# The norm sums of the input read from a second, token-major load, and the start of attention put in another order

## The chip, the cores and the metric

The kernel runs on one core of one Trainium2 chip. The metric is the device time of one execution in microseconds (us); the profile is one execution taken by the hardware profiler. The engines are TensorE (PE for its matmuls, PEld for its weight loads), VectorE (DVE), ScalarE (ACT), GpSimd (POOL) and SyncE (SP), which here only issues transfers. Each engine works through its instructions strictly in order; an instruction that waits holds back all behind it on that engine. A smaller time is better.

## The reference

One decoder block on a 1024 x 1024 input (1024 tokens, 1024 features), in float32:

```python
h = rmsnorm(x, g_mix_pre)                        # x * rsqrt(mean(x*x, -1) + 1e-6) * g
proj = h @ w_in + b_in                           # 512 pool | 512 q | 128 k | 128 v | 2048 gates
y_pool = multiscale_pool(u_pool, w_pool) * pool_scale      # windows 2, 4, 8, 16
q, k = partial_rotary(q), partial_rotary(k)      # first 16 of 64 dimensions of each head
y_attn = sliding_window_sink_attention(q, k, v)  # 8 query heads, 2 kv heads, window 128
merged = sigmoid(g0) * (y_pool @ w_branch_pool) + sigmoid(g1) * (y_attn @ w_branch_attn)
x = x + rmsnorm(merged @ w_out, g_mix_post)
x = x + rmsnorm(square(relu(rmsnorm(x, g_mlp_pre) @ w_up)) @ w_down, g_mlp_post)
```

Only the first two lines and the start of the attention matter for the change: `rmsnorm` needs, for each token, the sum of the squares of its 1024 features.

## The kernel before

**Precision.** A float32 operand is split into a high part (a cast to fp32r, on ACT) and a low part (the difference, on DVE); a product is then three matmul passes, high x high, high x low, low x high (`PASSES`, L32). `split` (L99) does both halves: its ACT cast is recorded as L101, its DVE subtraction as L104.

**The projection loop (L205 to L242).** x is loaded feature-major (`xt`, features on the partitions), 128 features per step k of 8. Step k loads `xs` (512 KB, four buffers of the tag `s4`) and 768 columns of weights `ws` (384 KB, three staging buffers `st`), multiplies `xs` by the gain and splits it (L227 on ACT, L228 on DVE, once for each half of the tokens), splits the query and the key/value weights, and multiplies: tokens 0 to 511, that is the token tiles n = 0 to 3 of 128 tokens, for the queries (`mm_q`, L183) and the keys and values (`mm_kv`, L192). That is 24 matmuls per step. The norm is not applied to x: the rows of the result are multiplied by the inverse root `r1` later. For it, each step also squares its `xs` in place on ACT (L235; step 0 writes the running sum `sq` directly, L233), and POOL adds the square to `sq` (L236; the last of the seven additions is on DVE). `xs` is free for the next load after that addition.

**After the loop (L722 on).** `sq` holds sums over 8 features for each partition; 16 small matmuls against a column of ones (L725, eight in the program, each recorded twice) finish the sum per token into `bss`, laced with the query matmuls of token tile 4. `rsqrt` (L106) makes `r1` from it. `pre_qkv(n)` (L255) then takes tile n out of PSUM with `r1` and the bias (L260, L261, DVE) and does the rotary part (L268 to L271: on DVE for n = 0, on POOL else). `post_qkv(n)` (L280) transposes it on PE (L289, L290) and splits it into query and key tiles for `score` (L312, matmuls L328). 

**What sets the order.** Up to L721 a scheduler with estimated times orders every engine. From L722 PE, DVE and ACT keep the written order, while the SP and POOL queues are still ordered by the scheduler. Between the pieces of the attention `fill(t)` (L643) takes t microseconds' worth, by estimate, of independent PE work from the generator `others` (L606): the query and key/value projections of the token tiles 4 to 7, then the pool branch's `u` projections (L574) and the product of `w_pool` with the branch weights (L594). `between` and `late` hold ACT and DVE work that belongs to that stream and is emitted at certain points of it. The stream takes its PSUM banks from three of the tag `mm`; token tile 5 gets the bank in which token tile 2's queries stood, so its first matmul needs `pre_qkv(2)`.

After the attention (about 178 us on) come the gate projections, the output projection, and the two MLP products, which the change does not touch.

Of the kernel before, what the change touches and what calls it, by code (L numbers as in the profile page):

```python
# [8 lines left out]
F32 = mybir.dt.float32  # L9
# [5 lines left out]
P = 128  # L15
S = 1024
# [26 lines left out]
V_BU = V_G + 8  # L43
V_BG = V_BU + 4
V_PS = V_BG + 16
V_ONE = V_PS + 4
V_N = V_ONE + 1


@with_exitstack  # L50
def block_kernel(ctx: ExitStack, tc, xt, x, consts, vecs, sinks, b_qkv, g_post, g_mlp, g_mlp_post,
# [94 lines left out]

    cst = cp.tile([P, C_N], F32, name="cst")
    vec = cp.tile([P, V_N], F32, name="vec")
    snk = cp.tile([P, NH], F32, name="snk")
    nsnk = cp.tile([P, NH], F32, name="nsnk")  # L150
    r1 = cp.tile([P, NT], F32, name="r1")
# [44 lines left out]
    bq01 = bank("sc", [2, 512])  # L196
    bq = {0: bq01[:, 0, :], 1: bq01[:, 1, :], 2: bank("mm"), 3: bank("mm")}
    bkv = {0: bank("at", [2, 256]), 2: bank("at", [2, 256])}
    bss = bank("at", [NT])
    bz = bank("mm")  # L200
    for j in range(11):
        pe.matmul(bz, zeros[:, 0, :P], zeros[:, 0, :], start=j == 0, stop=j == 10)
    sq = at("qkv", 3, [S])
    ones = vec[:, V_ONE:V_ONE + 1]
    for k in range(NK):  # L205
        xs = at("s4", 4, [S])
        ws = stage([768]) if k else ws_first
        if k < 2:
            nc.sync.dma_start(xs[:, :512], xt[k][:, :512])
            if k:  # L210
                nc.sync.dma_start(ws, w_qkv[k])
            else:
                nc.sync.dma_start(vec, vecs)
                nc.sync.dma_start(ws[:, 512:], w_qkv[k][:, 512:])
            nc.sync.dma_start(xs[:, 512:], xt[k][:, 512:])
        else:
            nc.sync.dma_start(xs, xt[k])
            nc.sync.dma_start(ws, w_qkv[k])
        halves_ = [xp.tile([P, 2, 512], F32R, tag="x", name=nm("x")) for _ in range(2)]
        gk = vec[:, V_G + k:V_G + k + 1]  # L220
        q = wslot([2, 512]) if k < 6 else ga_.tile([P, 2, 512], F32R, tag="ga", name=nm("wq"))
        if k % 2 == 0:
            wkv.append(ga_.tile([P, 2, 2, 256], F32R, tag="ga", name=nm("wkv")))
        kv = wkv[-1]
        for th, t in enumerate(halves_):
            c = slice(th * 512, (th + 1) * 512)
            act.activation(t[:, 0, :], xs[:, c], AF.Identity, scale=gk)  # L227
            dve.scalar_tensor_tensor(t[:, 1, :], xs[:, c], gk, f32(t[:, 0, :]), ALU.mult, ALU.subtract)  # L228
            if th == 0:
                split(q[:, 0, :], q[:, 1, :], ws[:, :512])  # L230
                split(kv[:, 0, k % 2, :], kv[:, 1, k % 2, :], ws[:, 512:])
        if k == 0:
            act.activation(sq, xs, AF.Square)  # L233
        else:
            act.activation(xs, xs, AF.Square)  # L235
            (pool if k < NK - 1 else dve).tensor_tensor(sq, sq, xs, ALU.add)  # L236
        xs_.append(halves_)
        wq.append(q)
        for n in range(4):
            mm_q(n, k, bq[n])  # L240
        for n in range(4):
            mm_kv(n, k, joint=True)  # L242
    nc.sync.dma_start(cst, consts)
    nc.sync.dma_start(snk, sinks.unsqueeze(0).broadcast_to([P, NH]))
    bq_b = bcast(b_qkv, 768)
# [290 lines left out]
    def flush(todo):  # L536
        while todo:
            todo.pop(0)()
# [67 lines left out]
    def others():  # L606
        for n in range(4, NT):
            flush(late)
            bq[n] = bank("mm")
            for k in range(NK):  # L610
                mm_q(n, k, bq[n])
                yield 3 * 0.227
            if n == NT - 1:
                load_u(3)
                flush(between[1])
            bkv[n] = bank("at" if n == 4 else "mm", [1, 256])
            for k in range(NK):
                mm_kv(n, k)
                yield 3 * 0.12
            if n == 4:  # L620
                late.append(lambda: pre_qkv(4))
            else:
                pre_qkv(n)
        wps = stage([4, P])
        nc.sync.dma_start(wps, w_pool)
        between[0].append(lambda: split(wpt[:, 0], wpt[:, 1], wps))
        wpt = bcp.tile([P, 2, 4, P], F32R, tag="bc", name="wpt")
        wpts.append(wpt)
        for gi in (3, 2, 1, 0):
            load_wb(gi)  # L630
            if gi:
                load_u(gi - 1)
            yield from u_half(gi, 0)
            if gi < 3:
                yield from wb_half(gi + 1, 1)
            yield from u_half(gi, 1)
            yield from wb_half(gi, 0)
        yield from wb_half(0, 1)
# [81 lines left out]

    LOW, HIGH = range(4), range(4, 8)  # L721
    with tc.manual_schedule(engines={mybir.EngineType.PE, mybir.EngineType.DVE, mybir.EngineType.Activation}):  # L722
        for n in range(NT):
            fill(0.34)
            pe.matmul(bss[:, n:n + 1], sq[:, n * P:(n + 1) * P], ones, start=n == 0, stop=n == NT - 1)  # L725
        rsqrt(r1, bss[:, :NT], NT)
        act.activation(warm, r1[:, :1], AF.Exp)
        pre_qkv(0)
        pre_qkv(1)
        fill(5.4)  # L730
        post_qkv(0)
        pre_qkv(2)
        fill(2.8)
        score(0, 0)
        score_prev(0, 0)
# [627 lines left out]
def _layout(inputs):  # L1363
# [18 lines left out]
    for col, t in ((C_COS, np.cos(ang)), (C_SIN, np.sin(ang))):  # L1382
# [4 lines left out]
        b_in[:512].reshape(4, P).T,  # L1387
        b_in[1280:].reshape(16, P).T,
        a["pool_scale"][0].reshape(4, P).T,
        np.ones((P, 1), f),  # L1390
    ], axis=1)
    return [
        ("xt", c(x.T).reshape(NK, P, S)),
# [39 lines left out]
```

## Time and profile before

| | us |
|---|---|
| median of 3 runs | 1133.97 (1133.69 to 1134.46) |
| the profiled execution, its own time | 1134.51 |
| its span from first to last instruction | 1132.7 |
| PE busy | 1114.8 |
| DVE busy | 820.6 |
| ACT busy | 526.7 |
| POOL busy | 77.8 |
| mean granted TensorE clock | 0.996 |

The span is 1.8 us shorter than the execution's time; what is saved inside the span is taken off the time. In a row of the timeline the first number is the start in us, the second the duration; `x12` means that twelve equal instructions were merged, and a bracket gives the idle time just before and what ended it. In a row of groups the numbers behind the bar are the total busy time in us, the mean in ns, and the idle time of the engine just before its members. Windows give, for a stretch, the busy time of each engine, the granted clock, the share of the transfer engines and GB/s. PE's busy time contains slow stretches and modelled ends, so starts of instructions are compared rather than busy shares.

### The profile page before, as it was taken

To read this page: it belongs to the slowest core of one execution; us is meant where nothing else is said; L and a number is where in the kernel's file an instruction comes from. 1 tells how busy PE (TensorE), PEld (TensorE's weight loads), DVE (VectorE), ACT (ScalarE), POOL (GpSimd) and SP (SyncE) were. 2 spreads that over 40 slices of the span, in tenths; PEclk is the share of its full clock that TensorE was granted. 3 is DMA by queue.
4 is the path that set the end of the run, shared out by engine and by line. 5 is a ranking of instruction groups with operands and counts; after the bars stand their busy time and mean duration, and the time that the engine had idled before them with its cause. 6 is when DMAs were issued, how large, how long until landed. Compare 5 with 4: busy or idle time off the path is not lost.

```text
span 1132.7 us, 14023 instructions
## 1 busy us (share of the span) xinstructions
PE 1114.8 (98%) x5183; PEld 920.9 (81%) x5183; DVE 820.6 (72%) x1210; ACT 526.7 (47%) x912; POOL 77.8 (7%) x111
## 2 busy tenths in 40 slices
PE   8999999999999999999999999999999999999997
PEld 7888778888888888888788888888888888888885
DVE  7668857899858885678998666666457955446787
ACT  6445655544432333446555444444444345344342
POOL 2443211000000330000000000000000000000000
PEclk9999999999999999999999999999999999999999
DMA  7205669366664444243365343434597765332652
GB/s 248 84 1 110 151 138 285 117 224 220 211 236 141 143 158 154 94 149 112 121 230 202 145 160 141 164 139 167 214 337 266 242 203 189 110 93 75 215 192 94
DMA packets 80179, 189.02 MB, mean 167 GB/s; under 512 B 6896, under 2 KB 19312, under 8 KB 80112
## 3 DMA queue, kind: packets, MB, share of 16 engines
q1 hardware_dynamic: 70144, 166.38, 43.8%
q10 hardware_dynamic: 5616, 19.66, 4.5%
q0 software_dynamic: 4352, 2.10, 1.8%
q8 instruction: 40, 0.66, 0.2%
q14 instruction: 27, 0.22, 0.1%
HBM read 132.54 MB, written 55.57 MB: 166 GB/s over the span
## 4 chain that ended last, share of the span: by engine, by line
PE 87%; DVE 7%; ACT 3%; DMA 2%; issue 1%; SPq 0%; DVEq 0%; ACTq 0%
PE mm L484 22%; PE at L484 16%; PE at L1270 14%; PE mm L1270 12%; PE mm L987 6%; PE mm L421 5%; PE mm L183 3%; PE mm L423 3%; PE mm L574 2%; PE at L987 1%; PE at L192 1%; DVE wh L104 1%; PE at L392 1%; PE sc L328 1%; DMA st<-in_w_up_dram 1%
## 5 line engine op out<-in xcount | busy, mean ns | idle before, releaser
L1270 PE MATMUL at<-ar,wh 128*128 128x512 f32 x744 | 169.6, 389 | 0.0
L1270 PEld LDWEIGHTS at<-ar,wh 128*128 128x128 f32 x744 | 139.6, 188 | 29.3 <-DVE ar L104 0.4
L1270 PE MATMUL mm<-ar,wh 128*128 128x512 f32 x576 | 131.0, 389 | 0.0
L1270 PEld LDWEIGHTS mm<-ar,wh 128*128 128x128 f32 x576 | 108.1, 188 | 22.5
L104 DVE TENSOR_TENSOR wh<-raw,wh 128x1024 fp32r<-128x1024 f32 x53 | 64.8, 1223 | 83.4 <-ACT wh L101 83.4
L101 ACT CAST wh<-raw 128x1024 fp32r<-128x1024 f32 x53 | 55.8, 1053 | 133.9 <-PE at L1270 60.3
L101 ACT CAST wh<-st 128x512 fp32r<-128x512 f32 (+1 forms) x105 | 66.3, 642 | 84.6 <-PE at L484 29.9
L104 DVE TENSOR_TENSOR wh<-st,wh 128x512 fp32r<-128x512 f32 (+1 forms) x105 | 81.8, 789 | 29.6 <-ACT wh L101 27.1
L484 PE MATMUL mm<-gr,wh 128*128 128x512 f32 x309 | 74.2, 390 | 0.0
L484 PE MATMUL mm<-T,wx 128*128 128x512 f32 x288 | 67.6, 389 | 0.0
L484 PEld LDWEIGHTS mm<-gr,wh 128*128 128x128 f32 x309 | 57.8, 188 | 11.8
L484 PEld LDWEIGHTS mm<-T,wx 128*128 128x128 f32 x288 | 54.1, 188 | 11.2
L484 PE MATMUL at<-T,wx 128*128 128x512 f32 x252 | 59.1, 389 | 0.0
L484 PEld LDWEIGHTS at<-T,wx 128*128 128x128 f32 x252 | 47.3, 188 | 9.8
L484 PE MATMUL mm<-x,wh 128*128 128x512 f32 x240 | 55.2, 389 | 0.0
L484 PEld LDWEIGHTS mm<-x,wh 128*128 128x128 f32 x240 | 45.1, 188 | 9.3
L104 DVE TENSOR_TENSOR ar<-B,ar 128x1024 fp32r<-128x1024 f32 x37 | 45.1, 1219 | 6.6 <-ACT ar L101 6.4
L574 PE MATMUL mm<-x,wh 128*128 128x512 f32 x192 | 47.6, 396 | 0.0
L101 ACT CAST ar<-B 128x1024 fp32r<-128x1024 f32 x37 | 38.9, 1050 | 8.8 <-DMA B<-in_w_dn_dram 6.0
L484 PE MATMUL at<-gr,wh 128*128 128x512 f32 x174 | 42.3, 390 | 0.0
L574 PEld LDWEIGHTS mm<-x,wh 128*128 128x128 f32 x192 | 35.2, 188 | 7.8
L484 PEld LDWEIGHTS at<-gr,wh 128*128 128x128 f32 x174 | 32.6, 188 | 7.2 <-DVE gr L104 0.5
(362 smaller groups left out, 2188.3 us busy)
## 6 DMA issues: line engine op xcount, KB each, us to landing
raw<-f_dram SPq DMA_DIRECT2D x53, 512.0 KB, 3.8
f_dram<-g SPq DMA_DIRECT2D x30, 512.0 KB, 3.3
B<-in_w_dn_dram SPq DMA_DIRECT2D x24, 512.0 KB, 6.6
st<-in_w_up_dram SPq DMA_DIRECT2D x22, 512.0 KB, 3.7
st<-in_w_g_dram SPq DMA_DIRECT2D x18, 512.0 KB, 4.2
f_dram<-g ACTq DMA_DIRECT2D x17, 512.0 KB, 2.6
g<-spill_dram SPq DMA_DIRECT2D x16, 512.0 KB, 4.4
raw<-in_w_dn_dram SPq DMA_DIRECT2D x16, 512.0 KB, 4.6
```

The source lines that it names most:

```text
L101: act.copy(hi, src)
L104: eng.tensor_tensor(lo, src, f32(hi), ALU.subtract)
L183: pe.matmul(bq, xs_[k][n // 4][:, xh, n % 4 * P:(n % 4 + 1) * P], wq[k][:, h, :], start=k == 0 and j == 0, stop=k == NK - 1 and j == 2)
L192: pe.matmul(bkv_of(n), xs_[k][n // 4][:, xh, n % 4 * P:(n % 4 + 1) * P], wkv[k // 2][:, h, k % 2, :], start=k == 0 and j == 0 and not (joi ...
L328: pe.matmul(sb[:, kv, i, :nk], qt[r, qx, m * P:(m + 1) * P], kx[r, k0:k0 + nk], start=j == 0, stop=j == 2)
L392: pe.matmul(flat(yb), v[:, kv, :], flat(p[:, 4 * kv:4 * kv + 4]), start=j == 0, stop=j == len(mms) - 1)
L421: pe.matmul(bs[th], whi[:, k, :], rhs(k, hl, th), start=k == 0 and hl == 0, stop=False)
L423: pe.matmul(bs[th], wlo[:, k, :], rhs(k, 0, th), start=False, stop=k == nk - 1)
L484: pe.matmul(b, w[:, wh, kt, :], xo[kt][:, xh, :], start=not after and kt == 0 and j == 0, stop=kt == 3 and j == 2, skip_group_check=after)
L574: pe.matmul(b, (whi, wlo)[h][:, k, :], xr(k, xh, th), start=j == 0, stop=j == len(mms) - 1)
L987: pe.matmul(obs[n][dj], l, wos[k][whl][:, dj * 512:(dj + 1) * 512], start=k == 0 and hl == 0 and whl == 0, stop=k == NK - 1 and hl == 1)
L1270: pe.matmul(bs[t], fo[fh][:, k2, t * P:(t + 1) * P], wo_[wh][:, k2, :], start=not after and s2 == 0 and k2 == 0 and j == 0, stop=s2 == NS ...
```

## The change

- The squares no longer come from `xs`. A new helper `token_square(n)` loads the 128 tokens of tile n once more, token-major (`x[n]`, 512 KB, on the SP queue, into one of three buffers of the tag `s8` that the scores use later), squares it in place on ACT, and lets ACT sum along the features into column n of a new tile `ssq`. It is called for tile k - 2 in step k from 2 on, and twice after the loop. The seven additions (six on POOL, one on DVE), the running sum `sq`, the sixteen matmuls against ones, their bank `bss` and the column of ones in `vec` go away. `xs` is no longer overwritten.
- `pre_qkv(2)` stands ahead of `post_qkv(0)`, and `fill(5.4)` after it becomes `fill(7.0)`. With the eight `fill(0.34)` that went with the small matmuls, the stream's share before `post_qkv(0)` is 7.0 instead of 8.12.
- The last pool weights (`load_u(3)`) are requested after token tile 6's queries instead of tile 7's, and their split is emitted after half of tile 7's query matmuls (k = 3) instead of after all of them.

In the built program the tiles outside this stage's own pool stand at the same addresses as before (`ssq` fits into the room that the shorter `vec` leaves); within the stage's pool the tags change places.

```diff
-V_ONE = V_PS + 4
-V_N = V_ONE + 1
+V_N = V_PS + 4
...
+    ssq = cp.tile([P, NT], F32, name="ssq")
...
-    bss = bank("at", [NT])
...
-    sq = at("qkv", 3, [S])
-    ones = vec[:, V_ONE:V_ONE + 1]
+
+    def token_square(n):
+
+        t = at("s8", 3, [D])
+        nc.sync.dma_start(t, x[n])
+        act.activation(t, t, AF.Square, accum_out=ssq[:, n:n + 1])
+
     for k in range(NK):
...
-        if k == 0:
-            act.activation(sq, xs, AF.Square)
-        else:
-            act.activation(xs, xs, AF.Square)
-            (pool if k < NK - 1 else dve).tensor_tensor(sq, sq, xs, ALU.add)
+        if k >= 2:
+            token_square(k - 2)
...
+    for n in (6, 7):
+        token_square(n)
     nc.sync.dma_start(cst, consts)
...
             for k in range(NK):
                 mm_q(n, k, bq[n])
+                if n == NT - 1 and k == 3:
+                    flush(between[1])
                 yield 3 * 0.227
-            if n == NT - 1:
+            if n == NT - 2:
                 load_u(3)
-                flush(between[1])
...
-        for n in range(NT):
-            fill(0.34)
-            pe.matmul(bss[:, n:n + 1], sq[:, n * P:(n + 1) * P], ones, start=n == 0, stop=n == NT - 1)
-        rsqrt(r1, bss[:, :NT], NT)
+        rsqrt(r1, ssq, NT)
         act.activation(warm, r1[:, :1], AF.Exp)
         pre_qkv(0)
         pre_qkv(1)
-        fill(5.4)
+        pre_qkv(2)
+        fill(7.0)
         post_qkv(0)
-        pre_qkv(2)
         fill(2.8)
```

How the built programs stand, at two places. Names carry a buffer number; line numbers are each program's own (L231, L232 of the changed kernel are L227, L228 of before; L100 is L101).

**ACT and SP in the projection loop.** ACT, step 3 with the square that follows, before and now (`x` is the split input, `wh` and `wkv` the weights, `s` an input buffer, or the token-major copy in the row of L207):

```order
L227 ACTIVATE x_249<-s_27_245,vec 128x512
L227 ACTIVATE x_250<-s_27_245,vec 128x512
L235 ACTIVATE s_21_203<-s_21_203 128x1024
L101 CAST wh_251<-st_246 128x512
L101 CAST wkv_210<-st_246 128x256
L235 ACTIVATE s_27_245<-s_27_245 128x1024
```

```order
L231 ACTIVATE x_246<-s_26_242,vec 128x512
L231 ACTIVATE x_247<-s_26_242,vec 128x512
L100 CAST wh_248<-st_243 128x512
L100 CAST wkv_206<-st_243 128x256
L207 ACTIVATE s_31_257,ssq<-s_31_257 128x1024
```

SP's requests of the same steps, now (before, the same rows without L206):

```order
L221 DMA s_19_199<-in_xt_dram 128x1024
L222 DMA st_200<-in_w_qkv_dram 128x768
L206 DMA s_25_215<-in_x_dram 128x1024
L221 DMA s_26_242<-in_xt_dram 128x1024
L222 DMA st_243<-in_w_qkv_dram 128x768
L206 DMA s_31_257<-in_x_dram 128x1024
```

Each step has one square as before, but it stands behind that step's casts and reads a buffer of its own; each step from k = 2 on requests 512 KB more on the same queue, behind its weights and ahead of the next step's input.

**PE and DVE from token tile 4's projections to the first scores.** PE before (`at_523` are tile 4's keys and values, `mm_580` tile 5's queries, `sc_548` the transposes of tile 0, `sc_594` its first scores):

```order
L192 MATMUL at_523<-wkv_376,x_374 128x256 x3
L192 MATMUL at_523<-wkv_376,x_416 128x256 x3
L289 MATMUL sc_548<-cst,qkv_495 128x128 x4
L290 MATMUL sc_548<-cst,qkv_495 128x128
L183 MATMUL mm_580<-wh_126,x_125 128x512 x3
L183 MATMUL mm_580<-wh_168,x_167 128x512 x3
L183 MATMUL mm_580<-wh_209,x_208 128x512 x3
L183 MATMUL mm_580<-wh_251,x_250 128x512 x3
L328 MATMUL sc_594<-klo_458,qt_554 128x128 x2
```

PE now (`at_531` are tile 4's keys and values):

```order
L192 MATMUL at_531<-wkv_291,x_289 128x256 x3
L292 MATMUL sc_547<-cst,qkv_482 128x128 x4
L293 MATMUL sc_547<-cst,qkv_482 128x128
L192 MATMUL at_531<-wkv_291,x_332 128x256 x3
L192 MATMUL at_531<-wkv_376,x_374 128x256 x3
L192 MATMUL at_531<-wkv_376,x_417 128x256 x3
L183 MATMUL mm_580<-wh_125,x_124 128x512 x3
L183 MATMUL mm_580<-wh_166,x_165 128x512 x3
L183 MATMUL mm_580<-wh_205,x_204 128x512 x3
L331 MATMUL sc_591<-klo_466,qt_553 128x128 x2
```

DVE between the second and the fifth token tile, before and now (`qkv_503` is tile 1, `y_564` and `y_498` tile 2, `qkv_572` tile 4; L104 and L103 split tile 0 for the scores):

```order
L261 SCALAR_TENSOR_TENSOR qkv_503<-at_103,r_86,bc_454 128x256
L104 TENSOR_TENSOR qt_554<-sc_548,qt_554 128x512
L104 TENSOR_TENSOR klo_458<-sc_548,khi_457 128x128
L260 SCALAR_TENSOR_TENSOR y_564<-mm_101,r_86,bc_454 128x512
L261 SCALAR_TENSOR_TENSOR y_564<-at_104,r_86,bc_454 128x256
L260 SCALAR_TENSOR_TENSOR qkv_572<-mm_462,r_86,bc_454 128x512
```

```order
L264 SCALAR_TENSOR_TENSOR qkv_490<-at_104,r_87,bc_462 128x256
L263 SCALAR_TENSOR_TENSOR y_498<-mm_102,r_87,bc_462 128x512
L264 SCALAR_TENSOR_TENSOR y_498<-at_105,r_87,bc_462 128x256
L103 TENSOR_TENSOR qt_553<-sc_547,qt_553 128x512
L103 TENSOR_TENSOR klo_466<-sc_547,khi_465 128x128
L263 SCALAR_TENSOR_TENSOR qkv_572<-mm_506,r_87,bc_462 128x512
```

Nine of the 24 key/value matmuls now stand behind the transposes and nine instead of twelve query matmuls of tile 5 follow them; on DVE the two instructions that read tile 2 stand ahead of the split that waits for the transposes. Through the rest of the attention the stream of filler stands some nine small matmuls less far at each piece than before, so that the casts and splits of the branch weights (in `load_u` and `load_wb`, `parts`) fall between other pieces of the attention.

1 line of the change is left out of this document (removed).

## The prediction

> **What bounds the kernel now.** I read the page's busy times and chain first, then PE's waits by stretch, then the timeline up to 61 us, where every line of the diff acts.
>
> ```profile
> PE 1114.8 (98%) x5183; PEld 920.9 (81%) x5183; DVE 820.6 (72%) x1210; ACT 526.7 (47%) x912; POOL 77.8 (7%) x111
> PE 87%; DVE 7%; ACT 3%; DMA 2%; issue 1%; SPq 0%; DVEq 0%; ACTq 0%
> PE sc L183 <- DVE wh L104: 1.8, 3, 0.7
> PE mm L183 <- DVE y L260: 2.7, 1, 2.7
> PE sc L328 <- DVE s L337: 0.6, 1, 0.6
> PE at L392 <- DVE qt L104: 1.0, 1, 1.0
> PE at L371 <- ACT yt L393: 0.6, 1, 0.6
> ```
>
> PE makes 87% of the chain, so time is gained where PE waits, works slowly or does needless work. Of the waits shown, 4.5 us (the first two, before 61 us) lie in the changed part; the other three are in the attention. Behind it the chain hands over from one stage to the next by what PE finished, so that a gain at the front should arrive at the end.
>
> In the projection loop the starts of a step's first matmul tell its length:
>
> ```profile
> 6.00 1.98 PE L183 MATMUL sc<-wh,x 128*128 128x512 f32 x6
> 10.62 0.47 PE L183 MATMUL sc<-wh,x 128*128 128x512 f32 x1
> 25.87 1.55 PE L183 MATMUL sc<-wh,x 128*128 128x512 f32 x6
> 42.59 0.86 PE L183 MATMUL mm<-wh,x 128*128 128x512 f32 x3
> 6.65 0.42 DVE L104 TENSOR_TENSOR wkv<-st,wkv 128x256 fp32r<-128x256 f32 x1
> 27.78 2.42 POOL L236 TENSOR_TENSOR qkv<-qkv,s 128x1024 f32<-128x1024 f32 x1 [3.79 <-ACT s L235]
> 27.97 2.52 DVE L104 TENSOR_TENSOR wkv<-st,wkv 128x256 fp32r<-128x256 f32 x1 [0.16 <-ACT wkv L101]
> L236 POOL TENSOR_TENSOR qkv<-qkv,s 128x1024 f32<-128x1024 f32 x6 | 14.8, 2461 | 24.3 <-ACT s L235 24.2
> L104 DVE TENSOR_TENSOR wkv<-st,wkv 128x256 fp32r<-128x256 f32 x8 | 11.8, 1476 | 0.5 <-ACT wkv L101 0.4
> L228 DVE SCALAR_TENSOR_TENSOR x<-s,vec,x 128x512 fp32r<-128x512 f32 x16 | 11.4, 743 | 2.2 <-ACT x L227 2.2
> L235 ACT ACTIVATE s<-s 128x1024 f32<-128x1024 f32 x7 | 7.4, 1061 | 10.5 <-DVE x L228 10.5
> ```
>
> The last four steps take (42.59 - 25.87) / 4 = 4.18 us each, in which PE has no wait. Steps 1 to 3 take (25.87 - 10.62) / 3 = 5.08. What is late there is DVE's split of the weights, and what makes it late is POOL: a split that takes 0.42 us alone takes 2.52 beside an addition of 2.42 and ends with it, eight of them average 1.476, and the six additions hold 14.8 us in all. DVE's own work is about 2 x 0.74 + 0.69 + 0.42 = 2.6 us a step, well under 4.18.
>
> Behind the loop:
>
> ```profile
> 43.28 0.50 PE L725 MATMUL at<-vec,qkv 128*128 128x1 f32 x4
> 47.20 2.87 PE mm L183 x12
> 49.91 3.04 PE L192 MATMUL at<-wkv,x 128*128 128x256 f32 x24
> 52.79 0.60 PE L289 MATMUL sc<-cst,qkv 128*128 128x128 f32 x4
> 53.22 0.27 PE L290 MATMUL sc<-cst,qkv 128*128 128x128 f32 x1
> 55.38 0.74 DVE L260 SCALAR_TENSOR_TENSOR y<-mm,r,bc 128x512 f32<-128x512 f32 x1
> 56.17 4.54 PE L183 MATMUL mm<-wh,x 128*128 128x512 f32 x12 [2.68 <-DVE y L260]
> 60.65 0.33 PE L328 MATMUL sc<-klo,qt 64*128 64x128 f32 x2
> 56.20:60.70 4.50, 4.50 (x14) 3.33 (x14) 1.36 (x3) 0.00 (x0) 4.03 (x11) 0.64 0.00 0
> ```
>
> The transposes of tile 0 end at 53.49. PE then idles until 56.17, because the bank of tile 5's queries is read out only at 55.38, behind the split that itself waits for the transposes. And the next twelve matmuls take 4.48 us (to 60.65) where twelve took 2.87 (47.20 to 50.08): the window has a granted clock of 0.64 there.
>
> **The change part by part**, measured at one event, the first score matmul, with twelve query matmuls of tile 5 done ahead of it; now 60.65.
>
> *Additions gone.* Steps 1 to 3 fall from 5.08 to 4.18: (5.08 - 4.18) x 3 = 2.7 us. Least: the listed waits, 1.8.
>
> *Squares moved to a second load.* ACT still has eight squares of 1.06; they lose the wait for DVE (10.5 us of idle in all). The sum over a row adds an accumulator read that this stage does not show; the softmax's own exponentials have one:
>
> ```profile
> 69.01 0.19 ACT L354 ACTIVATION_READ_ACCUMULATOR s<-s,nmx 128x1 f32 x1
> L227 ACT ACTIVATE x<-s,vec 128x512 fp32r<-128x512 f32 x16 | 10.9, 715 | 1.5 <-DMA s<-in_xt_dram 1.5
> L101 ACT CAST wh<-st 128x512 fp32r<-128x512 f32 x6 | 3.6, 606 | 2.0 <-DMA st<-in_w_qkv_dram 2.0
> L101 ACT CAST wkv<-st 128x256 fp32r<-128x256 f32 x8 | 3.2, 394 | 0.0
> 0.00:15.00 15.00, 12.90 (x55) 10.09 (x56) 7.04 (x13) 9.91 (x17) 1.61 (x5) 1.00 0.85 298
> 10.00:15.00 5.00, 4.62 (x27) 3.86 (x26) 3.96 (x6) 4.63 (x10) 1.41 (x1) 1.00 0.99 393
> 24.30:42.60 18.30, 18.30 (x111) 16.30 (x110) 16.54 (x18) 10.23 (x15) 7.22 (x3) 1.00 0.55 180
> ```
>
> A step costs ACT 2 x 0.715 + 0.606 + 0.394 + 1.061 + 0.19 = 3.7 us, under 4.18, so it is hidden behind PE as long as the loads keep up; each late load would now hold the next step's casts behind its square. The loads grow from 0.92 to 1.44 MB a step (512 + 384 + 512 KB), on SP's queue ahead of the next step's input: 345 GB/s for 4.18 us. The queue moved 393 GB/s in 10 to 15 us with all transfer engines busy (0.99); the 180 of the later stretch is at a share of 0.55, a queue that waits for buffers. The requests wait for staging buffers as now, freed by DVE's splits, which come earlier, and from the fourth token tile on for a square. By 15 us 15 x 0.298 = 4.5 MB are in; steps 0 to 3 and two token tiles are 4.7 MB, and step 3 is wanted on PE at 10.62 + 2 x 4.18 = 19.0. Step 7's weights close 10.0 MB, due at 15 + 5.5 / 0.393 = 29, against PE's 35.7. Cost taken: 0; without that cover, see the rivals.
>
> *Is r1 in time?* All 11.5 MB are in by about 33 us at 393 GB/s, 36 at 345. Then
>
> ```profile
> 41.62 1.28 ACT L109 ACT_TABLE_LOAD   x1
> 47.24 0.27 ACT L109 ACTIVATE sm<-at,eps 128x8 f32<-128x8 f32 x1 [4.34 <-PE at L725]
> 48.66 0.75 DVE L260 SCALAR_TENSOR_TENSOR qkv<-sc,r,bc 128x512 f32<-128x512 f32 x1
> 50.69 0.23 DVE L271 TENSOR_TENSOR qkv<-qkv,rb 128x80 f32<-128x80 f32 x1
> ```
>
> the last square with its read, 1.25, the table load, which no longer hides behind PE's sums, 1.28, and from the root to r1 1.42 (47.24 to 48.66) give 37 to 40 us. Tile 0 is ready 2.26 later, and not before the loop's last product at 39.9, so by about 42.5. PE asks for it behind 24 query and 15 key/value matmuls, 39.9 + 5.7 + 1.8 = 47.4. Some 5 us of slack.
>
> *Sixteen small matmuls gone.* From 42.59 to 49.91 PE did 24 query matmuls (2 x 2.87 = 5.74) and these: 7.32 - 5.74 = 1.6 us. Tile 4's 24 key/value matmuls, 49.91 to 52.79, stay at 2.88.
>
> *Tile 2 read ahead of the split.* The bank of tile 5's queries is free by about 45 us (tile 1 and tile 2, an L260 of 0.74 and a shorter L261 each), and PE wants it near 49: the wait of 2.7 us goes. Late next is tile 0's split for the scores, 1.9 us from the last transpose (53.49) to the L260 that stands right behind it (55.38); 9 key/value and 9 query matmuls (9/24 x 2.88 + 9/12 x 2.87 = 3.2) cover it.
>
> *The clock.* With no such gap the twelve matmuls take 2.87 instead of 4.48: 1.6 us. Bounds 0 and 1.6. The row comes first: a 2.7 us gap was followed by 0.64. [...]
>
> *Last u weights.* The request moves by one tile, the split by half of one. The trace shows no PE wait for them (none on an L574 matmul), so 0.
>
> *Later order.* Weight splits fall between other pieces of the attention. Its three waits sum to 2.2 us; that bounds what can be won. What can be lost:
>
> ```profile
> 144.38 1.16 ACT L560 ACTIVATE wh<-st,vec 128x1024 fp32r<-128x1024 f32 x1
> 145.57 1.29 DVE L561 SCALAR_TENSOR_TENSOR wh<-st,vec,wh 128x1024 fp32r<-128x1024 f32 x1 [3.77 <-ACT wh L560]
> ```
>
> one such pair ahead of a piece's casts, 2.5 us, less the slack there. I take 0 between +2.2 and -2.5.
>
> The sum: 10.62 + 7 x 4.18 = 39.88; + 5.74 (queries) + 2.88 (keys, values) + 0.70 (transposes, 52.79 to 53.49) + 2.87 (twelve of tile 5) = 52.07; against 60.65 that is 8.6 us (2.7 + 1.6 + 2.7 + 1.6). On the profiled execution's own 1134.5 it gives 1125.9. That execution lies 0.5 above the median of the runs, so for a median I forecast **1125.4 us**.
>
> **The rivals.**
>
> *Loads starve PE (slower).* If the queue gives less than 345 GB/s, the loop follows the transfers, since ACT's squares wait for them in order. Step 7's weights then land at 15 + 5.5 / rate and PE ends about 5.5 us later (1.3 for cast and split, 4.18). All 8.6 us are gone when that end is at 48.5, weights at 43: a rate of 200 GB/s. At the 180 of 24 to 43 us it is 45.6 + 5.5 = 51.1, a net loss of 2.6: 1136.6. For it: longer queues and an ACT that now waits for two loads a step. Against it: 393 GB/s where the queue was full.
>
> *Attention takes part back.* DVE and ACT, not PE, set the pace of two or three pieces there (the waits above), and the weight scaling now falls into others. Two such pairs uncovered: 5 us, 1130.4.
>
> *The clock is not won.* Another gap, or a median without the dip: 8.6 - 1.6 = 7.0, 1127.
>
> *The loop does not speed up*, because ACT or the loads pace it at 5.08 a step in place of DVE: 8.6 - 2.7 and nothing for steps 4 to 7 (4 x 0.9 lost): 2.3 us, 1131.7.
>
> **How the numbers follow.** Forecast 0.57 (1123.5 to 1127), clock not won 0.11, attention takes back 0.14, loop not faster 0.08, starved 0.06, nothing anywhere or something unseen 0.04. Range 1123.5 to 1130.5: the low end is the sum with most of the attention's waits won; the high end has 1.8 for the loop, no clock and one uncovered pair, 1.8 + 1.6 + 2.7 - 2.5 = 3.6. A difference can be told from no change at 0.2%, 2.3 us: the loop rival lies on that line and counts half. Faster 0.86, within 0.07, slower 0.07.
>
> **What would show it.** In the changed profile: steps of 4.18 us from 10.6 on; the first query matmul of tile 4 near 40; DVE splits of 0.42 and 0.69, no POOL work before 40; no PE wait for y L263; granted clock 1.00 from 45 to 62; the first scores near 51. Wrong if steps stay near 5, if ACT's L231 or L207 rows show idle time ended by transfers, if PE waits for the transposes' input, or if the first scores are at 51 and the waits in the attention grow by several us.

## The result, and the profile after

The changed kernel takes 1124.87 us (median of 6 runs, 1124.43 to 1125.69), the kernel before, beside it, 1133.83 (1132.05 to 1134.46): a ratio of 0.9924, 95% interval 0.9911 to 0.9937, 9.0 us by the medians. Forecast were 1125.4, range 1123.5 to 1130.5. The profiled execution took 1125.69 with a span of 1123.8, against 1134.51 and 1132.7.

Busy times and chain on the page of the changed kernel:

```profile
PE 1111.3 (99%) x5167; PEld 917.5 (82%) x5167; DVE 807.2 (72%) x1209; ACT 528.5 (47%) x920; POOL 62.3 (6%) x105
PE 90%; DVE 6%; ACT 2%; issue 1%; DMA 1%; DVEq 0%
```

PE does 3.5 us less and its share of the chain rises to 90%. PE's timeline from the second step of the loop to the first scores (start, duration):

```profile
10.65 1.53 PE L183 MATMUL sc<-wh,x 128*128 128x512 f32 x6
...
35.71 1.55 PE L183 MATMUL sc<-wq,x 128*128 128x512 f32 x6
...
39.89 4.27 PE L183 MATMUL mm<-wh,x 128*128 128x512 f32 x18
44.00 1.52 PE L183 MATMUL mm<-wq,x 128*128 128x512 f32 x6
45.36 1.96 PE L192 MATMUL at<-wkv,x 128*128 128x256 f32 x15
47.15 0.60 PE L292 MATMUL sc<-cst,qkv 128*128 128x128 f32 x4
...
48.77 2.23 PE L183 MATMUL mm<-wh,x 128*128 128x512 f32 x9
50.92 0.33 PE L331 MATMUL sc<-klo,qt 64*128 64x128 f32 x2
```

All steps are 4.18 us long ((39.89 - 10.65) / 7), and no row carries a wait. Tile 4's queries start at 39.89 (before 42.59, forecast 39.88). The first score matmul stands at 50.92 with nine matmuls of tile 5 ahead of it instead of twelve; three more at 2.15 / 9 make it 51.64, against 60.65: 9.0 us, the whole difference. The same by windows (busy time of PE, its weight load, DVE, ACT, POOL; then granted clock, transfer share, GB/s):

```profile
10.00:15.00 5.00, 5.00 (x32) 4.57 (x32) 4.00 (x7) 4.37 (x9) 0.00 (x0) 1.00 1.03 416
20.00:25.00 5.00, 5.00 (x29) 4.36 (x28) 3.35 (x6) 3.90 (x8) 0.00 (x0) 1.00 1.03 404
25.00:30.00 5.00, 5.00 (x29) 4.38 (x28) 2.89 (x6) 4.49 (x9) 0.00 (x0) 1.00 1.03 407
45.00:62.00 17.00, 16.64 (x132) 14.14 (x131) 7.94 (x14) 7.59 (x27) 11.27 (x30) 1.00 0.01 1
```

POOL is idle in the loop, PE is full, the loads run at 404 to 416 GB/s, and the clock behind the loop is 1.00, where the window of before had 0.64. What PE still waits for after the start:

```profile
PE at L395 <- DVE qt L103: 1.5, 1, 1.5
PE at L487 <- DVE f_first L519: 1.1, 1, 1.1
PE sc L331 <- DVE s L340: 0.4, 1, 0.4
```

The attention (L395, L331) has 1.9 us of waits in place of the 2.2 that the page showed before. (L487, in a later stage, waited about as long before, 1.0 us on its L484.)

One of the signs that the prediction named for being wrong did show: between 9 and 40 us ACT waits for transfers.

```profile
ACT x L231 <- DMA s<-in_xt_dram: 1.4, 2, 1.0
ACT s L207 <- DMA s<-in_x_dram: 0.6, 2, 0.4
```

It cost nothing, since ACT and DVE work ahead of PE: the split of the last step's weights is done at 33.1, and PE takes them at 35.71.

### The profile page after: what moved, and what is told of

Read it like the earlier page. It is cut to its first block, busy times and chain, and to the rows that moved or that the text cites. A ratio compares the mean times of both kernels' runs of the same rounds, so it can differ in the third digit from the quotient of the medians.

```text
span 1123.8 us, 13993 instructions
## 1 busy us (share of the span) xinstructions
PE 1111.3 (99%) x5167; PEld 917.5 (82%) x5167; DVE 807.2 (72%) x1209; ACT 528.5 (47%) x920; POOL 62.3 (6%) x105
## 4 chain that ended last, share of the span: by engine, by line
PE 90%; DVE 6%; ACT 2%; issue 1%; DMA 1%; DVEq 0%
PE mm L487 23%; PE at L487 16%; PE at L1271 14%; PE mm L1271 12%; PE mm L988 6%; PE mm L424 5%; PE mm L183 3%; PE mm L426 3%; PE mm L577 2%; PE at L192 1%; PE sc L183 1%; PE at L988 1%; PE at L395 1%; PE sc L331 1%; PE mm L192 1%
## 5 line engine op out<-in xcount | busy, mean ns | idle before, releaser
L103 DVE TENSOR_TENSOR wh<-raw,wh 128x1024 fp32r<-128x1024 f32 x53 | 64.9, 1224 | 83.6 <-ACT wh L100 83.5
L100 ACT CAST wh<-raw 128x1024 fp32r<-128x1024 f32 x53 | 55.8, 1053 | 133.7 <-PE at L1271 61.2
L100 ACT CAST wh<-st 128x512 fp32r<-128x512 f32 (+1 forms) x105 | 66.2, 641 | 79.8 <-PE at L487 29.8
L103 DVE TENSOR_TENSOR wh<-st,wh 128x512 fp32r<-128x512 f32 (+1 forms) x105 | 78.3, 756 | 30.3 <-ACT wh L100 28.0
L487 PE MATMUL mm<-gr,wh 128*128 128x512 f32 x309 | 74.6, 391 | 0.1
L487 PEld LDWEIGHTS mm<-gr,wh 128*128 128x128 f32 x309 | 57.7, 188 | 12.3 <-ACT g L1053 0.5
L487 PE MATMUL mm<-T,wx 128*128 128x512 f32 x288 | 67.6, 389 | 0.0
L487 PEld LDWEIGHTS mm<-T,wx 128*128 128x128 f32 x288 | 54.1, 188 | 11.2
L487 PE MATMUL at<-T,wx 128*128 128x512 f32 x252 | 59.1, 389 | 0.0
L487 PEld LDWEIGHTS at<-T,wx 128*128 128x128 f32 x252 | 47.3, 188 | 9.8
L487 PE MATMUL mm<-x,wh 128*128 128x512 f32 x240 | 55.2, 389 | 0.0
L487 PEld LDWEIGHTS mm<-x,wh 128*128 128x128 f32 x240 | 45.0, 188 | 9.4
L103 DVE TENSOR_TENSOR ar<-B,ar 128x1024 fp32r<-128x1024 f32 x37 | 45.1, 1220 | 6.8 <-ACT ar L100 6.5
L100 ACT CAST ar<-B 128x1024 fp32r<-128x1024 f32 x37 | 38.9, 1050 | 9.0 <-DMA B<-in_w_dn_dram 6.1
L487 PE MATMUL at<-gr,wh 128*128 128x512 f32 x174 | 42.4, 390 | 0.0
L487 PEld LDWEIGHTS at<-gr,wh 128*128 128x128 f32 x174 | 32.6, 188 | 7.3 <-DVE gr L103 0.5
```

Source lines behind the costliest of these rows:

```text
L100: act.copy(hi, src)
L103: eng.tensor_tensor(lo, src, f32(hi), ALU.subtract)
L487: pe.matmul(b, w[:, wh, kt, :], xo[kt][:, xh, :], start=not after and kt == 0 and j == 0, stop=kt == 3 and j == 2, skip_group_check=after)
```

## The experiments

Twelve kernels were measured in four groups of four, four, two and two, in the order of this section. The kernels of a group ran on one chip, beside the kernel before, and each group had another chip. Medians of the kernel before in the four groups: 1134.36, 1133.89, 1132.65, 1132.62. Where groups are compared, this is done by ratios to them or by traces. A ratio comes from all runs of both kernels and can differ from the quotient of the medians, here by up to 0.0008; its 95% interval is in brackets.

### The order alone

```diff
 (kernel before)
         pre_qkv(1)
+        pre_qkv(2)
         fill(5.4)
         post_qkv(0)
-        pre_qkv(2)
```

> The kernel before with one thing of the change: tile 2 is taken out of PSUM ahead of tile 0's split (pre_qkv(2) in front of fill(5.4)). The norm sums, their additions on POOL and the small matmuls stay, and so do all fill amounts. Theory of the prediction: the PE wait of 2.7 us for y goes, and the slow twelve matmuls after it (4.48 instead of 2.87) with it: 2.7 + 1.6 = 4.3 us, 1133.8 -> 1129.5, first scores near 56.4 instead of 60.65, granted clock 1.00 from 50 to 60. Rival, the slow clock does not hang on the gap: only 2.7 us, 1131.1, and the window still shows a clock near 0.64. Rival, the order is worth nothing and the whole gain comes from the norm: 1133.8.

Measured: 1128.88 (1128.82 to 1129.06), ratio 0.9960 (0.9945 to 0.9974). PE's timeline of it:

```profile
52.66 0.27 PE L290 MATMUL sc<-cst,qkv 128*128 128x128 f32 x1
52.69 3.00 PE L183 MATMUL mm<-wh,x 128*128 128x512 f32 x12
55.62 0.33 PE L328 MATMUL sc<-klo,qt 64*128 64x128 f32 x2
```

The twelve matmuls follow the transpose at once and take 3.00 instead of 4.54; its windows from 40 to 60 us have a clock of 1.00. The gain is 4.5 us by the ratio (2.9 to 6.2 by its interval) and 5.5 by the medians, no less than the 4.3 of the theory. Both rivals fall: one asked for a gain of 2.7 and a clock near 0.64, the other for no gain.

### The norm alone

```diff
 (changed kernel)
         pre_qkv(1)
-        pre_qkv(2)
-        fill(7.0)
+        fill(8.12)
         post_qkv(0)
+        pre_qkv(2)
```

> The changed kernel with the order of before behind the loop (pre_qkv(2) behind post_qkv(0), 8.12 us of filler ahead of it). The token-major loads and ACT's sums stay. Theory of the prediction: the loop keeps its 4.18 us a step and the small matmuls stay away (2.7 + 1.6 = 4.3 us against the kernel before), while the wait of some 2.7 us for y and the slow matmuls behind it come back: 1129.5, and a window with a granted clock near 0.64 again at about 51 to 56 us. Rival, the clock fell in the kernel before for another reason than the gap: 1127.9 and a clock of 1.00. Rival, the order in the attention pays, not the start: 1133.8, since the fill amounts are those of before.

Measured: 1131.83 (nine runs, 1129.02 to 1133.09), ratio 0.9979 (0.9968 to 0.9990). The loop is 4.18 a step, and behind it:

```profile
48.50 0.27 PE L293 MATMUL sc<-cst,qkv 128*128 128x128 f32 x1
51.45 4.32 PE L183 MATMUL mm<-wh,x 128*128 128x512 f32 x12 [2.68 <-DVE y L263]
55.70 0.47 PE L331 MATMUL sc<-klo,qt 64*128 64x128 f32 x2
```

The window in the slow stretch:

```profile
52.90:56.20 3.30, 3.30 (x13) 2.15 (x12) 0.00 (x0) 0.00 (x0) 3.22 (x10) 0.50 0.00 0
```

The wait and the slow matmuls are back, as expected. The first scores come 5.0 earlier than before, but by the ratio only 2.4 us are won, less than the 4.3 expected. The nine runs lie 4.1 us apart; the profiled one took 1130.45, the second shortest and 4.1 less than the profiled execution of the kernel before. Why the other runs win less stays open. This was followed up with a kernel that keeps PE busy in that wait (below).

### POOL's additions put back

```diff
 (changed kernel, junk = at("qkv", 3, [S]))
+        if k == 0:
+            pool.tensor_copy(junk, xs)
+        elif k < NK - 1:
+            pool.tensor_tensor(junk, junk, xs, ALU.add)
         if k >= 2:
             token_square(k - 2)
```

> The changed kernel with one copy and six additions of 128 x 1024 on POOL put back into steps 0 to 6 of the loop, on a running tile that nothing reads; the output does not depend on them. Orders of PE, ACT, DVE and SP are the same. Theory of the prediction (DVE's splits are held up by POOL's additions of 2.4 us): DVE's splits beside them take about 2.5 us again, its step grows from 2.6 to about 5.0, and 1.8 to 4 us are lost in the loop: 1126.7 to 1128.9, likeliest 1127.6. Rival, the steps of before were late because of ACT's squares and their wait, not because of POOL: no loss, 1124.9, splits of 0.42 and 0.69. Rival, the additions were late because they waited for the square: they start earlier here and collide less, about 1 us lost, 1126.

Measured: 1134.84 (1132.63 to 1135.46), ratio 1.0004 (0.9994 to 1.0013). By the ratios 9.1 us are lost, over twice the upper end of the expectation. The timelines of POOL, DVE and PE, of POOL and DVE also one instruction alone:

```profile
9.81 8.10 POOL L240 TENSOR_TENSOR qkv<-qkv,s 128x1024 f32<-128x1024 f32 x3 [2.03 <-DMA s<-in_xt_dram]
12.69 2.47 POOL L240 TENSOR_TENSOR qkv<-qkv,s 128x1024 f32<-128x1024 f32 x1
...
12.82 8.41 DVE L233 SCALAR_TENSOR_TENSOR x<-s,vec,x 128x512 fp32r<-128x512 f32 x3
12.82 2.89 DVE L233 SCALAR_TENSOR_TENSOR x<-s,vec,x 128x512 fp32r<-128x512 f32 x1
...
21.88 2.50 PE L183 MATMUL sc<-wh,x 128*128 128x512 f32 x5 [6.79 <-DVE wh L103]
24.18 2.73 PE L183 MATMUL mm<-wh,x 128*128 128x512 f32 x6
```

Three additions follow each other and a fourth comes 0.25 us later, and three DVE operations of 0.75 take 8.41 us. The first of them starts 0.13 us behind an addition of 2.47 and ends 0.55 us after it, at 15.71; the other two lie in the same way beside the next two additions. PE waits 6.79 for the weights' split behind them and then works slowly (six matmuls in 2.73 instead of 1.52; granted clock 0.50 from 20 to 25 us). Tile 4's queries start at 49.08 in place of 39.89: the whole loss, 9.2 us, arises in the loop, 6.8 of it as the wait and 2.4 by the clock. So the mechanism is the predicted one, and stronger: if the DVE operation runs at its usual pace once the addition has ended, 0.20 of its 0.75 us were done in the 2.34 us beside it (an estimate, 0.75 - 0.55). The expectation had only the splits in the way of the additions and no fall of the clock. In the kernel before, 24.2 of the 24.3 us in which POOL idled ahead of its additions ended with ACT's square; that this kept them apart, and the damage at 2.7 us, is a reading of the two traces.

### A third load per tile

```diff
 (changed kernel, token_square)
         act.activation(t, t, AF.Square, accum_out=ssq[:, n:n + 1])
+        extra = at("qkv", 3, [D])
+        pool.tensor_copy(extra[:, :1], ssq[:, n:n + 1])
+        nc.gpsimd.dma_start(extra, x[n])
```

> The changed kernel with a third 512 KB load for each token tile, issued on POOL's queue once that tile's square is done, into a buffer that nothing reads; the output does not depend on it. Orders of PE, ACT, DVE and SP are the same. The loop then wants 1.96 MB per 4.18 us, 470 GB/s, where the trace of the changed kernel shows about 405 with all transfer engines busy. Theory, the loads have room left but not this much: the last weights come near 36 us instead of 28, PE's last step slips by 0 to 3 us, likeliest 1.5: 1126.4. Rival, the loads already pace the loop of the changed kernel (each extra byte costs at once): 4.2 MB at 405 GB/s is 10 us, most of it lost: above 1131. Rival, there is ample room, because tiles are loaded several steps ahead: 1124.9.

Measured: 1130.79 (1127.38 to 1131.5), ratio 0.9970 (0.9957 to 0.9982). Most of this loss is the experiment's own: tile 0 uses a buffer of the same tag, and DVE waits there for the extra load. One of its windows, with the transfers at their limit (last two columns):

```profile
30.00:35.00 5.00, 4.44 (x25) 3.49 (x24) 2.67 (x5) 4.38 (x8) 1.24 (x3) 1.00 1.03 409
```

Its timelines, of PE and then of DVE:

```profile
33.22 1.45 PE L183 MATMUL sc<-wq,x 128*128 128x512 f32 x5 [0.44 <-DVE wq L103]
...
41.50 4.27 PE L183 MATMUL mm<-wh,x 128*128 128x512 f32 x18
...
51.76 1.12 PE L295 MATMUL sc<-cst,qkv 128*128 128x128 f32 x4 [2.85 <-DVE qkv L266]
...
48.79 0.75 DVE L266 SCALAR_TENSOR_TENSOR qkv<-sc,r,bc 128x512 f32<-128x512 f32 x1 [3.63 <-DMA qkv<-in_x_dram]
```

What the loads cost is read at 41.50: 1.6 us over 39.89, as the theory had it (1.5). The wait of 2.85 at 51.76 and the slow transposes behind it come from the buffer. So the changed loop has room, about 405 GB/s against the 345 that it asks for, and 4.2 MB more cost it 1.6 us in this trace.

### More filler ahead of the attention

```diff
 (changed kernel)
-        fill(3.7)
+        fill(4.8)
         for n in range(NT):
```

> The changed kernel with fill(3.7) ahead of the attention loop at 4.8, which gives the stream back the 1.12 us that it lost ahead of post_qkv(0): from there on weight casts, splits and scalings fall into the same pieces of the attention as in the kernel before. Theory of the prediction (the later order is worth about 0): the 1.5 us wait for tile qt goes or moves, the three waits of 2.2 us of the kernel before come back, 1124.9 becomes 1124.5 to 1125.7. Rival, the gain of the changed kernel comes in part from the new places of the scalings: 2 us or more are lost, 1127.

Measured: 1125.16 (1124.26 to 1126.01), beside 1125.37 (1124.78 to 1126.42) for the changed kernel in the same group. The wait for qt falls from 1.5 to 1.0, but the three waits of the kernel before (2.2 us) do not all come back: 1.0 and 0.3 are left. The total moves by less than the runs differ, so no worth of the later order shows.

### The last u weights as before

```diff
 (changed kernel)
                 mm_q(n, k, bq[n])
-                if n == NT - 1 and k == 3:
-                    flush(between[1])
                 yield 3 * 0.227
-            if n == NT - 2:
+            if n == NT - 1:
                 load_u(3)
+                flush(between[1])
```

> The changed kernel with the last u weights requested and split where the kernel before does it. Theory of the prediction (worth 0, since no PE wait hangs on them): 1124.9 within 0.5, and no wait of PE on u's matmuls. Rival, the weights come late with the shorter start: PE waits 1 us or more on u's first matmul, 1126 or more.

Measured: 1129.47 (1128.36 to 1130.42), 4.1 us over the changed kernel beside it. The theory (0) falls. ACT's and PE's timelines:

```profile
88.73 0.39 ACT L357 ACTIVATE s<-s,nmx 128x128 f32<-128x128 f32 x1
...
90.27 1.03 ACT L100 CAST wh<-st 128x1024 fp32r<-128x1024 f32 x1
...
91.35 1.20 PE L577 MATMUL mm<-x,wh 128*128 128x512 f32 x4 [2.27 <-ACT wh L100]
92.39 0.94 PE L395 MATMUL at<-s,v 128*128 128x512 f32 x2
93.12 1.05 PE L395 MATMUL at<-s,dv 128*128 128x512 f32 x2
```

The cast of the weights stands behind four exponentials on ACT, PE waits 2.27 us for it, and the next matmuls take 1.05 where they take 0.61 to 0.62 in the changed kernel, which has that cast at 82.08, ahead of these exponentials. From 92.60 to 95.80 the granted clock is 0.50. The rival is right, but its sign (a wait of 1 us or more) was less than half of the loss.

### Tile's split ahead of the maximum

```diff
 (changed kernel, loop of the attention)
                 score_prev(n + 2, 1)
-                softmax_max(n + 2)
             if n + 3 < NT:
                 post_qkv(n + 3)
+            if n + 2 < NT:
+                softmax_max(n + 2)
```

> The changed kernel with DVE's order altered in the attention: the split of the next token tile (post_qkv(n + 3)) stands ahead of softmax_max(n + 2) instead of behind it, in all pieces where both exist. Orders of PE and ACT stay. Theory: the 1.5 us wait of PE on an attention bank ends with the split of qt, which stands behind a maximum of 1.22 and two small operations; ahead of them the split comes 1.5 us earlier and the wait goes: 1123.4, with the exponentials 1 us later but nothing waiting for them. Rival, the later maximum delays the exponentials and the wait moves to the transposes of the next piece: 1124.9 or 1 us more.

Measured: 1128.14 (eight runs, 1126.85 to 1131.12), 2.8 over the changed kernel beside it. PE's waits from 60 to 170 us:

```profile
PE at L374 <- ACT yt L396: 3.4, 3, 2.6
```

The wait for qt is gone, and a longer one has come in its place: the later maximum holds up the exponentials, ACT's copies of yt stand behind them, and PE waits for their bank. The rival has the mechanism right; its price, 1 us at most, was too low.

### The changed kernel again

> The changed kernel as it is, beside the three runs that are compared with it: 1124.9 by its earlier runs, within 0.6.

Measured: 1125.37 (1124.78 to 1126.42), ratio 0.9931 (0.9916 to 0.9946). The result repeats; this is the run that the three before it are compared with.

### Order, and the additions on DVE

```diff
 (kernel of "The order alone")
-            (pool if k < NK - 1 else dve).tensor_tensor(sq, sq, xs, ALU.add)
+            dve.tensor_tensor(sq, sq, xs, ALU.add)
```

> The kernel of the order-only experiment, and all seven additions of the norm on DVE instead of six on POOL: no second load of x, squares and small matmuls as in the kernel before. Theory (POOL's additions alone made the steps late; DVE has room, 2.6 us a step and one addition of about 1.1 against 4.18): the waits of 0.69 and 0.75 for wh go, the loop gets the 2.1 us shorter by which the changed kernel's is shorter, and only the small matmuls are left between it and the changed kernel: 1128.9 - 2.1 = 1126.8, splits of 0.42 and 0.69. Rival, ACT's squares and their wait for DVE made the steps late: 1128.9, steps of about 5 as before. Rival, one more operation on DVE a step makes DVE late itself: 1130.

Measured: 1127.68 (1126.98 to 1127.85), ratio 0.9951 (0.9937 to 0.9966). DVE's groups up to 45 us (total busy us and mean ns behind the bar):

```profile
L236 DVE TENSOR_TENSOR qkv<-qkv,s 128x1024 f32<-128x1024 f32 x7 | 8.6, 1222 | 1.3 <-ACT s L235 1.3
L104 DVE TENSOR_TENSOR wkv<-st,wkv 128x256 fp32r<-128x256 f32 x8 | 3.4, 419 | 0.0
```

PE's timeline:

```profile
10.67 0.39 PE L183 MATMUL sc<-wh,x 128*128 128x512 f32 x1
...
40.37 0.86 PE L183 MATMUL mm<-wh,x 128*128 128x512 f32 x3
...
47.70 3.03 PE L192 MATMUL at<-wkv,x 128*128 128x256 f32 x24
```

DVE does an addition in 1.22 where POOL needs 2.4, and all splits take 0.42 again. Tile 4's queries start at 40.37 (42.02 in the kernel it was made from), without the second load and with ACT's squares as they were: POOL's additions were the cause. The trace decides this: the intervals of the two ratios (0.9951 and 0.9960) overlap. That is 1.65 us of the 2.1 expected, since the steps are still 4.24 on average. The small matmuls remain, 7.33 us from 40.37 to 47.70 against 5.47 in the changed kernel, 1.9 us.

### A smaller gap

```diff
 (changed kernel)
         pre_qkv(1)
-        pre_qkv(2)
         fill(7.0)
         post_qkv(0)
+        pre_qkv(2)
```

> The changed kernel with only the place of pre_qkv(2) undone (behind post_qkv(0)); the filler ahead of it stays 7.0, so that 9 key/value matmuls of 1.15 us cover part of the wait for tile 2's bank, which falls from 2.7 to about 1.5 us. Theory by the rows so far (a wait of 1.5 in the attention left the granted clock at 1.00, waits of 2.7 and 2.9 brought it to about 0.64): only the wait is lost, 1126.4, runs as close together as those of the kernels without a gap (0.3 to 1.3 us). Rival, the clock answers to any gap in part: 1127 to 1128, a clock below 1 from 50 to 56 us, and runs several us apart. Rival, the wait is covered by what stands around it: 1124.9.

Measured: 1127.64, ratio 0.9956 (0.9939 to 0.9973). The four runs are 1126.62, 1126.72, 1128.56 and 1128.93. The profiled one is the first: PE waits 1.6 us for y, and the clock is 1.00 in all windows. No expectation holds for all four: two runs lose no more than the wait, two lose 2 us more, and of these two there is no trace.

### The gap kept busy

```diff
 (kernel of "The norm alone", kv4[0] with room for 512)
         post_qkv(0)
+        for j in range(20):
+            pe.matmul(kv4[0][:, 0, 256:], xs_[j % 8][1][:, 0, :P],
+                      wkv[j % 8 // 2][:, 0, j % 2, :], start=True, stop=True)
         pre_qkv(2)
```

> The kernel of the norm-only experiment, in which PE waits 2.7 us for tile 2's bank, with 20 key/value matmuls of tile 4 done once more inside that wait (about 0.12 us each, 2.4 us, into a spare half of tile 4's key/value bank that nothing reads). PE gets its bank no earlier; it is only not idle. Orders of ACT, DVE, POOL and SP are the same. Theory, the clock falls because PE is idle, and it is this fall that costs the rest and makes the runs differ: the granted clock stays 1.00 from 40 to 60 us, first scores near 54.1 instead of 55.7, only the wait is lost against the changed kernel (2.5 to 3 us), 1127.9, and the runs lie within 1.8 us of each other instead of 4.1. Rival, the clock falls because of something else there (load of the other engines, the order): about 0.64 again, 1131, runs 4 us apart.

Measured: 1128.9 (1128.44 to 1129.67), ratio 0.9964 (0.9950 to 0.9978). PE's timeline:

```profile
48.80 2.62 PE L740 MATMUL at<-wkv,x 128*128 128x256 f32 x20
51.72 3.02 PE L183 MATMUL mm<-wh,x 128*128 128x512 f32 x12 [0.30 <-DVE y L263]
54.67 0.33 PE L331 MATMUL sc<-klo,qt 64*128 64x128 f32 x2
```

The window around it:

```profile
50.00:60.00 10.00, 9.70 (x68) 7.84 (x68) 5.68 (x11) 2.15 (x6) 7.70 (x18) 1.00 0.00 0
```

PE gets its bank no earlier, but the twelve matmuls behind the wait take 3.02 instead of 4.32, the clock is 1.00, and the runs lie 1.2 us apart instead of 4.1. So twenty matmuls of no use win 1.3 us in the traces, and 1.7 by the ratios (0.9964 against 0.9979, whose intervals overlap). This speaks for PE's idleness as what lowers the clock, but it is one execution, and the runs say less than it seems: in this group the kernel before, which has the gap, shows a mean clock of 0.998 or 0.999 in seven of nine runs, where the first group had 0.995 to 0.998. The order alone, in the first group, speaks more clearly: without the gap all four runs have 0.998 or 0.999. The last section has a third sign. The time is 1.0 over the 1127.9 expected. Against the kernel of the next experiment, in the same group, 4.3 us are lost; 2.9 of them are the wait (2.62 + 0.30), and the attention's waits are those of the kernel before again, 2.2 us in place of 1.6.

### Weight work behind the casts

```diff
 (changed kernel, loop of the attention)
             attend_t(n)
+            held[0] = False
+            while len(held) > 1:
+                flush(between[held.pop()])
...
             attend_v(n)
-            held[0] = False
-            while len(held) > 1:
-                flush(between[held.pop()])
```

> The changed kernel with the held weight work of the stream (copies of wt, scaling of w_bp, splits of u weights) emitted behind the next piece's attend_t instead of ahead of it. PE's order stays. In the piece with the 1.5 us wait, ACT's casts for the attention then stand ahead of a copy of 0.58 and a scaling of 1.15, and DVE can start its splits near 119.2 instead of 121.7. Theory, DVE's queue sets this piece and starts 1.3 us earlier: the wait for qt falls to about 0.2, 1125.1 becomes 1123.8. Rival, the weight work is then late for the stream's own matmuls, or another piece gets the wait: 1125 to 1127, with a PE wait on an L577 or L597 matmul or on a transpose.

Measured: 1124.61 (1124.19 to 1124.93), ratio 0.9925 (0.9911 to 0.9938), the same as the changed kernel. DVE's timeline in that piece:

```profile
119.65 1.29 DVE L103 TENSOR_TENSOR s<-at,s 128x512 fp32r<-128x512 f32 x2 [2.58 <-ACT s L100]
121.68 1.28 DVE L564 SCALAR_TENSOR_TENSOR wh<-st,vec,wh 128x1024 fp32r<-128x1024 f32 x1 [0.73 <-ACT wh L563]
122.88 0.73 DVE L340 COPY_PREDICATED s<-cst,sc 128x512 f32<-128x512 uint32 x1
...
131.39 0.68 DVE L103 TENSOR_TENSOR qt<-at,qt 128x512 fp32r<-128x512 f32 x1
```

The splits do start 2.0 us earlier (121.69 in the changed kernel), but DVE then waits 0.73 for the scaling, which is late in its turn, and from 122.88 on stands where it stood (122.89). The wait for qt falls by 0.2. No version tried beats the changed kernel beyond what runs differ.

## Why the prediction was right, point by point

The time, the sign and the sum came out: 8.6 us forecast at the first score matmul, 9.0 in the trace.

*Additions gone* (2.7): tile 4's queries start 42.59 - 39.89 = 2.70 earlier. That POOL held up DVE is shown twice: putting the additions back brings a delay back (9.2 us in the loop), and taking them to DVE ends it (splits of 0.42 again) with no other part of the change but the order behind the loop. With the additions put back, a DVE operation of 0.75 takes 2.89 beside an addition of 2.47 and ends 0.55 us after it. By what means an addition on the one engine holds up the other is not shown.

*Squares moved to a second load* (0): right. The queue held 404 to 416 GB/s where 345 were needed, and ACT was busy 3.9 to 4.8 of 5 us without setting the pace. The rival of starving loads lost all 8.6 us only at 200 GB/s, and the queue never came near that while it was full; with 470 GB/s asked for, 1.6 us went. That ACT would show no wait for transfers was too strict a sign: it waited, and PE did not.

*Is r1 in time?* (5 us of slack): r1 is done at 38.6 and tile 0 at 41.0; PE asks at 47.15, so 6.2.

*Sixteen small matmuls gone* (1.6): from 39.89 to 45.36 are 5.47, against 7.32: 1.85. This is most of the 0.4 by which the sum was short. The step had taken the 24 queries at 2.87 a dozen; without the interruptions they need 2.74. The rest is the transposes, 0.47 (47.15 to 47.62) where the sum has 0.70, since key/value matmuls follow them at once.

*Tile 2 read ahead of the split* (2.7): the wait is gone, and tile 0's split is covered as said. In the order alone, too, the wait is gone whole.

*The clock* (1.6, bounds 0 and 1.6): right for the two profiled executions, with some luck in which ones were profiled: the runs of the kernel before lie 3.9 us apart in the first group, at mean clocks of 0.995 to 0.998, and the step took the loss as one number, with a rival for its absence. What it took for a clock of 0.64 is 0.50 for 3.4 us (last section), half of which is 1.7 us. The kernel with PE kept busy in the gap won 1.3 us in the traces and 1.7 by the ratios; single runs of the kernels with a gap lie up to 4 us apart.

*Last u weights* (0): wrong as a statement on the edit. The step argued from a trace in which PE did not wait for them; but the change takes 1.12 us of filler away ahead of them, and with the old request the cast falls behind four exponentials and costs 4.1 us. The forecast did not suffer, since the edit was in it. Without this edit the change wins 4.2 (ratio 0.9963, 0.9950 to 0.9976) instead of the 7.8 of the same group (0.9931).

*Later order* (0, between +2.2 and -2.5): right as far as it was tried. With the 1.1 us of filler given back the time was the same (1125.16 and 1125.37).

The parts together: the ratios of the order alone and the norm alone give 4.5 and 2.4, 6.9 us in sum, each known to about 1.5; both at once give 8.6. That a part is worth more when the other is there cannot be told from their sum within these intervals.

## What to carry to other kernels

An operation that looks cheap on its own engine (2.4 us on idle POOL) is to be priced by what it stops on the engine beside it (a split of 0.42 took 2.52); here taking it to the busier DVE at 1.2 us already brought the end of the loop 1.65 us forward. A short wait of PE costs more than its length when the clock falls behind it (in the kernel before 2.68 us of wait, and half of 3.4 us at a clock of 0.50), and the runs of such a kernel scatter (here 2.1 to 4.3 us); a wide spread of runs is itself a hint to look for gaps, here of 2.3 us and more, and in one kernel of 1.6. When filler ahead of a stage is shortened, look at every piece of work that was in time only because of it, in the new order and not in the old trace.

## What was not expected of the hardware

The mean granted clock of one and the same kernel differs from one execution to the next: in the kernel before, whose trace has a gap of 2.7 us, 0.995 to 0.998 in the twenty runs of the first group and 0.996 to 0.999 in the nine of the last. That the clock falls behind the gap in some executions and not in others is a reading of these numbers; no pair of traces shows it. Kernels (4 to 20 runs each) whose longest PE wait after the start was 1.5 us or less had runs within 0.2 to 1.8 us of each other (order alone 0.2, weight work behind the casts 0.7, additions on DVE 0.9, gap kept busy 1.2, the changed kernel 1.3 and 1.6, more filler 1.8). With longer waits the runs spread: 1.6 us of wait, 2.3 apart; 2.3 (old u request), 2.1; 2.6 (split ahead of the maximum), 4.3; 2.7 (norm alone), 4.1; 2.9 (third load), 4.1; 6.8 (additions put back), 2.8; and 2.7 in the kernel before, 3.9 in its twenty runs of the first group (4.1, 2.3 and 2.7 in its twelve, seven and nine of the others). The numbers of runs differ, and a spread grows with them. In the twenty the shortest span was 1130.2 us at a mean granted clock of 0.998, the longest 1134.0 at 0.995; 0.003 of 1132 are 3.4 of the 3.8 us. Single runs depart from this (1133.9 at 0.997).

How far the clock falls behind a gap is the same in the five profiled executions that show it. Read in short windows, it is 0.50 for 3.4 us in the kernel before (56.1 to 59.5), the norm alone (52.9 to 56.3), the third load (51.1 to 54.5) and the old u request (92.5 to 95.9), and for 6.8 us with the additions put back; values between, like 0.64, are means over stretches that lie partly outside. In the kernel before:

```profile
56.10:59.40 3.30, 3.23 (x8) 2.55 (x9) 1.46 (x4) 0.00 (x0) 2.81 (x8) 0.50 0.00 0
```

In the norm alone the fall comes 1.4 us after PE has taken up work again (51.45). At the end of the profiled executions of the kernel before and of the changed kernel PE only idles, and the clock falls to 0.50 some 2.3 and 2.1 us after its last matmul. This is the third sign for PE's idleness as the cause.

In the profiled execution with the split ahead of the maximum even a wait of 2.6 us left the clock at 1.00; PE's timeline there:

```profile
135.78 0.66 PE L374 MATMUL at<-cst,s 128*128 128x128 f32 x4 [2.56 <-ACT yt L396]
```

The window behind the wait:

```profile
135.00:140.00 5.00, 4.22 (x28) 3.44 (x29) 3.27 (x5) 4.80 (x17) 1.02 (x1) 1.00 0.52 149
```

So a wait of 2.6 us was followed by a clock of 1.00, and waits of 2.3 (old u request) and 2.7 (the kernel before, the norm alone) by 0.50; what decides between them is not shown. That a wait of 1.6 already lowers it is suggested by the two pairs of runs 2 us apart, but no trace shows it.
